# Order of the gate's low-part products and a narrower form of the step-size products in a two-layer decoder kernel

## Chip, cores, metric

The kernel runs on one core of one Trainium2 chip. The metric is the device time of one execution in microseconds; a kernel's time is the median of several runs.

## What is computed

Two layers over 256 tokens of width 1024, in float32, weights used once:

```python
x = x + 0.5 * swiglu(rmsnorm(x, norm_w[l, 0]), gate, up, down)    # hidden 2816
h = rmsnorm(x, norm_w[l, 1])
x = x + mamba2_mixer(h, ...)          # layer 0;  zxbcdt = h @ w_in, the last 32 columns are dt
x = x + swa_sink_attention(h, ...)    # layer 1
x = x + 0.5 * swiglu(rmsnorm(x, norm_w[l, 2]), gate, up, down)
...
dt = softplus(dt_raw + dt_bias)       # step sizes of the 32 heads
```

## The kernel before

Activations stand transposed: eight tiles of 128 features by 256 tokens. Each float32 operand is split into a high part (rounded to float32r) and a low part (the rest, also float32r), and a product is made of three: high by high, high weight by low activation, low weight by high activation. `xs[k]` holds both activation parts side by side, 512 columns: `xh` is the first 256, `xl` the rest. Norm weights are folded into `xs`; the norm's own factor `rs` per token is applied after the products.

Weights come in units of 128 x 1024 (`ORDER` lists all 341 in their order of use). For each, ScalarE writes the high part `hi` (`Weights.high`, L144) and the vector engine the low part `lo` (`Weights.low`, L155). `tick()`, at the end of each unit, first runs what is due in this slot (`Slots`), and then has the parts made up to four units ahead.

A feed-forward stage (f0 to f3, 22 loop steps of 128 hidden columns each, called f) takes per f a gate unit `g`, an up unit `u` and, from f = 4, the down unit `d` of f - 4; the last two down units go together in `tail`. A gate or up unit is `wide`: eight products of 512 columns, high weight by `xs[k]`, and eight of 256 columns, low weight by `xh[k]`, all summed in one PSUM bank; the high weight's product with `xl` is in the bank's second half, and `add` (L514, L515) folds it: ScalarE copies the second half, the vector engine adds the first. In f = 0 the products alternate, in all other f (`by_part`) eight of the one kind follow eight of the other. A down unit (`rows`, L384) is 24 products of 256 columns into the four banks `da`. In f2 two units of the shared K (tile `kab`, 48 products of 256 columns) stand between u and d of f = 5.

At a stage's end `next_stage` updates the residual `X` part by part, ScalarE makes `xh`, the vector engine `xl` (L396), and `rs_stats`, `rs_diag`, `rs_spread` make the norm's factor with small products (tile `st`) between the first units.

The mixer (`ssm`) begins with the unit `dt`: 32 weight columns in a unit of 128, as 24 products of 256 columns in `unit`, in the half of a bank that it shares with the unit B0. `dt_chain` follows in slots: d0 scales it (`dt_raw`), d1 turns it to tokens by rows (`dtt`), d2 and d3 make softplus on four engines, d4 the running sums (`cst`).

Of the kernel before, what the change touches and what calls it, by code (L numbers as in the profile page):

```python
# [9 lines left out]
F32 = mybir.dt.float32  # L10
F32R = mybir.dt.float32r
I32 = mybir.dt.int32
AF = mybir.ActivationFunctionType
ALU = mybir.AluOpType
PSUM = bass.MemoryType.PSUM

P = 128
T = 256
D = 1024
KT = D // P  # L20
# [10 lines left out]
HEADS = 32  # L31
# [44 lines left out]
ORDER = order()  # L76
# [33 lines left out]
class Weights:  # L110
# [38 lines left out]
    def low(self, half=None):  # L149
        u = self.cut  # L150
        c, i = divmod(u, CH)
        if not half:
            self.lo = self.parts.tile([P, D], F32R, tag="lo", name=f"lo{u}")
        hi, lo, s = self.ready.get(u, self.hi), self.lo, self.piece(half)
        self.nc.vector.tensor_tensor(lo[:, s], self.chunks[c][:, i, s], hi[:, s].bitcast(F32), ALU.subtract)  # L155
        if half == 0:
            return
        self.ready[u] = (hi, lo)
        self.cut += 1
        if i == CH - 1 or u == NU - 1:  # L160
            del self.chunks[c]
            self.load()
# [53 lines left out]
class Trunk:  # L216
# [136 lines left out]
            before()  # L353
        self.tick()

    def wide(self, what, out, by_part=False):


        hi, lo = self.W.next(what)
        passes = [(k, w, x, n) for k in range(KT) for w, x, n in ((hi, self.xs, 2 * T), (lo, self.xh, T))]  # L360
        if by_part:
            passes = passes[0::2] + passes[1::2]
        for n, (k, w, x, c) in enumerate(passes):
            self.nc.tensor.matmul(  # L364
                out[:, 0:c], w[:, k * P : (k + 1) * P], x[k],
                start=n == 0, stop=n == len(passes) - 1, skip_group_check=True,
            )
        self.tick()
# [110 lines left out]
    def ffn(self, l, i, key, nxt):  # L479
        nc, wk = self.nc, self.fw  # L480
        self.stage_norm(key)
        accs = self.accs(f"da_{key}")
        hs = {}

        def evac(f, g, u):
            hh = self.op.tile([P, T], F32R, tag="high", name=f"hh_{key}_{f}")
            hl = self.op.tile([P, T], F32R, tag="low", name=f"hl_{key}_{f}")
            hs[f] = (hh, hl)

            def e0():  # L490
                nc.vector.tensor_tensor(g, g, self.rs, ALU.mult)
                nc.scalar.activation(g, g, AF.Silu)
                nc.vector.tensor_tensor(u, u, self.rs, ALU.mult)

            def e1():
                nc.vector.tensor_tensor(u, u, g, ALU.mult)
                nc.scalar.activation(hh, u, AF.Copy)

            def e2():
                nc.vector.tensor_tensor(hl, u, hh.bitcast(F32), ALU.subtract)  # L500

            wait = max(0, 4 - f) if key == "f0" else 2 if f == 0 else 0
            self.slots.chain(wait, [e0, e1, e2])

        def product(name, f, t):

            b = self.bank(f"{name}_{key}_{f}")
            if self.W.pos == 0:
                self.slots.at(0, lambda: nc.scalar.copy(t, b[:, 0:T]))
                self.unit((name, l, i, f), b[:, 0:T])  # L510
                return

            def add():
                nc.scalar.copy(t, b[:, T:])  # L514
                nc.vector.tensor_tensor(t, b[:, 0:T], t, ALU.add)  # L515

            self.slots.at(0, add)
            self.wide((name, l, i, f), b, by_part=f > 0)

        for f in range(NF):  # L520
            g, u = (wk.tile([P, T], F32, tag=n, bufs=4, name=f"{n}s_{key}_{f}") for n in "gu")
            product("g", f, g)
            evac_now = lambda: evac(f, g, u)
            self.slots.late(0, evac_now)
            product("u", f, u)
            if l == 1 and i == 0 and f == 0:
                self.split_k()
            if l == 1 and i == 0 and f == 5:
                self.shared_k()
            if f >= LAG:  # L530
                self.down(l, i, f - LAG, hs, accs)
        for f in range(NF - LAG, NF - 2):
            self.down(l, i, f, hs, accs)
        self.tail([(("d", l, i, f), *hs.pop(f)) for f in (NF - 2, NF - 1)], accs, nxt)
# [15 lines left out]
    def ssm(self, nxt):  # L550
        nc, tc, wk, sl = self.nc, self.tc, self.sw, self.slots
        V, A, G = nc.vector, nc.scalar, nc.gpsimd
        self.stage_norm("ssm")
        causal, ident = self.cc("causal"), self.ident
        H = HEADS
# [6 lines left out]
        def side(name):  # L562

            if sl.now < base + at["so", 0] - 2:
                return self.ps.tile([P, 512], F32, tag="acc", name=name)
            return self.bank(name)
# [3 lines left out]
        yh, yl, sq, R = {}, {}, {}, {}  # L570

        def half():
            if st["n"] % 2 == 0:
                st["bank"] = self.bank(f"sb{st['n']}")
            o = st["bank"][:, (st["n"] % 2) * T : (st["n"] % 2) * T + T]
            st["n"] += 1
            return o
# [28 lines left out]
        def dt_chain(o, d):  # L606

            f = lambda n: wk.tile([P, 2, H], F32, bufs=1, name=n)
            u, t, e, q, p = f("dt"), f("dt_t"), f("dt_e"), f("dt_q"), f("dt_p")
            raw = wk.tile([H, T], F32, bufs=1, name="dt_raw")  # L610
            an = wk.tile([P, H], F32, bufs=1, name="an")
            cs = wk.tile([H, 3 * P], F32, bufs=1, name="cs")
            tok = wk.tile([P, 2, H], F32, bufs=1, name="tok")
            st["dt"], st["tok"] = u, tok

            def d0():
                V.tensor_tensor(raw, o[:H], self.rs[:H], ALU.mult)

            def d1():
                b = st["b"] = side("dtt")  # L620
                for n in range(2):
                    nc.tensor.transpose(b[:, n * H : n * H + H], raw[:, n * P : n * P + P], ident[:H, :H])

            def d2():
                V.tensor_tensor(
                    u, st["b"][:, 0 : 2 * H].rearrange("p (b h) -> p b h", b=2),
                    self.s("dtb", 0, H).unsqueeze(1).broadcast_to([P, 2, H]), ALU.add,
                )
                A.activation(t, u, AF.Abs)
                A.activation(e, t, AF.Exp, scale=-1.0)  # L630
                A.activation(an, self.s("alog", 0, H), AF.Exp)

            def d3():
                G.tensor_scalar(t, e, 2.0, None, ALU.add)
                V.reciprocal(t, t)
                G.tensor_tensor(t, t, e, ALU.mult)
                G.tensor_tensor(q, t, t, ALU.mult)
                V.tensor_scalar(p, q, 2.0 / 15.0, None, ALU.mult)
                for c in (13, 11, 9, 7, 5, 3):
                    V.scalar_tensor_tensor(p, p, 2.0 / c, q, ALU.add, ALU.mult)  # L640
                V.tensor_scalar(p, p, 2.0, None, ALU.add)
                G.tensor_tensor(p, p, t, ALU.mult)
                G.tensor_scalar(u, u, 0.0, None, ALU.max)
                G.tensor_tensor(u, u, p, ALU.add)
                G.tensor_tensor(e, u, an.unsqueeze(1).broadcast_to([P, 2, H]), ALU.mult)
                G.tensor_scalar(e, e, -1.0, None, ALU.mult)

            def d4():
                b = st["b2"] = side("cst")
                for n in range(2):  # L650
                    nc.tensor.matmul(b[:H, n * P : n * P + P], e[:, n], causal, start=True, stop=True)
                for n in range(2):
                    nc.tensor.matmul(b[:, T + n * H : T + n * H + H], causal, e[:, n], start=True, stop=True)
                A.activation(cs[:, 0:P], b[:H, 0:P], AF.Copy, scale=-1.0)
                A.activation(cs[:, T:], b[:H, P:T], AF.Copy, scale=-1.0)
                A.activation(cs[:, P:T], b[:H, P:T], AF.Identity, bias=cs[:, P - 1 : P], scale=-1.0)
                nc.sync.dma_start(scratch, cs)
                A.copy(tok, b[:, T : T + 2 * H].rearrange("p (b h) -> p b h", b=2))

            sl.chain(d, [d0, d1, d2, d3])  # L660
            sl.at(d + 6, d4)

# [162 lines left out]
        for what in seq[:-2]:  # L825
            if what[0] == "so":
                tt = what[1]
                if not accs:
                    accs = self.accs("sa")
                self.rows([(self.W.next(what), yh[tt], yl[tt])], accs, tt == 0, False)  # L830
                self.tick()
            else:
                o = half()
                self.unit(what, o, before=lambda: evac(what, o, E[what] - at[what]), fresh=what == ("dt",))
# [402 lines left out]
```

## Time and profile before

| | |
|---|---|
| three runs, median (lowest to highest) | 1038.58 us (1037.32 to 1039.66) |
| the profiled execution, its own time | 1038.29 us |
| its span, first to last instruction | 1036.5 us, so 1.79 us lie around it |
| busy: PE, vector engine (DVE), ScalarE (ACT), GpSimd (POOL) | 1013.4, 774.7, 627.4, 79.5 us |
| chain that ended last, by line | up 23%, gate 22%, down 22% of the span |
| stages f0, mixer, f1, f2, attention, f3 begin at about | 8, 196, 393, 577, 766, 842 us |

A row of the timeline is a start in us, a length in us, the engine, the line and the operation with output and inputs, and how many were merged into it. A product's record reaches beyond the start of the next one, since products are pipelined: the distance of two starts is what a product costs in a row of products, and the record's length is more.

### The profile page before, as it was taken

How to read it: one execution, taken by the hardware profiler on the slowest of the kernel's cores; microseconds unless marked ns; L12 is line 12 of the kernel's file. 1: busy time of each engine (PE TensorE's matmuls, PEld its weight loads, DVE VectorE, ACT ScalarE, POOL GpSimd, SP SyncE). 2: the span in 40 equal slices, each digit the busy share in tenths (PEclk: the TensorE clock that was granted, in tenths of full speed). 3: DMA queues.
4: the chain of work that ended last, by engine and by line, in shares of the span. 5: the costliest groups of instructions: out<-in, count | busy, mean ns of one | idle time of the engine just before them, and what ended most of it. 6: DMA issues, size and time to landing. Idle time of an engine off the chain costs nothing.

```text
span 1036.5 us, 18344 instructions
## 1 busy us (share of the span) xinstructions
PE 1013.4 (98%) x7290; PEld 939.2 (91%) x7290; DVE 774.7 (75%) x1420; ACT 627.4 (61%) x1106; POOL 79.5 (8%) x122
## 2 busy tenths in 40 slices
PE   8999999999999999999999999999999999999996
PEld 7899999999989898999999899999998888999996
DVE  4866666888999968766667796666679877666665
ACT  6655555678886856555555664555565776555554
POOL 3000000210111112000000200000022020000000
PEclk9999999999999999999999999999999999999998
DMA  8555555547546354555455455555544335545531
GB/s 306 198 203 198 172 203 192 179 177 267 192 153 224 130 199 160 196 198 202 169 203 201 160 203 202 179 200 194 199 181 152 113 141 201 185 181 204 189 117 41
DMA packets 30132, 190.84 MB, mean 184 GB/s; under 512 B 3904, under 2 KB 5728, under 8 KB 8544
## 3 DMA queue, kind: packets, MB, share of 16 engines
q1 hardware_dynamic: 30048, 189.69, 51.5%
q8 instruction: 57, 0.93, 0.3%
q14 instruction: 27, 0.22, 0.1%
HBM read 187.27 MB, written 1.10 MB: 182 GB/s over the span
## 4 chain that ended last, share of the span: by engine, by line
PE 80%; DVE 12%; ACT 3%; DMA 2%; POOL 1%; issue 1%; SPq 0%; DVEq 0%; POOLq 0%
PE u_f L364 23%; PE g_f L364 22%; PE da_f L384 22%; PE sa L384 3%; PE sb L351 3%; DVE lo L155 2%; DVE xs L396 2%; PE aa L384 1%; DMA csb<-cs_scratch 1%; PE q L351 1%; DVE xs L603 1%; DVE X L404 1%; ACT hi L144 1%; DVE E L725 1%; ACT E L720 1%
## 5 line engine op out<-in xcount | busy, mean ns | idle before, releaser
L155 DVE TENSOR_TENSOR lo<-raw,hi 128x1024 fp32r<-128x1024 f32 (+1 forms) x343 | 414.9, 1213 | 15.2 <-ACT hi L144 15.2
L144 ACT ACTIVATE hi<-raw 128x1024 fp32r<-128x1024 f32 (+1 forms) x343 | 357.0, 1046 | 18.6 <-PE da_f L384 5.0
L384 PE MATMUL da_f<-hh_f,hi 128*128 128x256 f32 x704 | 194.3, 276 | 0.0
L384 PE MATMUL da_f<-hh_f,lo 128*128 128x256 f32 x704 | 194.3, 276 | 0.0
L384 PE MATMUL da_f<-hl_f,hi 128*128 128x256 f32 x704 | 194.3, 276 | 0.0
L364 PE MATMUL u_f<-xs,hi 128*128 128x512 f32 x704 | 181.2, 395 | 0.0
L364 PE MATMUL g_f<-xs,hi 128*128 128x512 f32 x696 | 176.6, 392 | 0.8 <-DVE xs L396 0.8
L364 PEld LDWEIGHTS u_f<-xs,hi 128*128 128x128 f32 x704 | 127.1, 188 | 22.4
L364 PEld LDWEIGHTS g_f<-xs,hi 128*128 128x128 f32 x696 | 124.5, 188 | 23.9 <-DVE xs L396 2.2
L384 PEld LDWEIGHTS da_f<-hl_f,hi 128*128 128x128 f32 x704 | 132.1, 188 | 0.0
L384 PEld LDWEIGHTS da_f<-hh_f,hi 128*128 128x128 f32 x704 | 132.1, 188 | 0.0
L384 PEld LDWEIGHTS da_f<-hh_f,lo 128*128 128x128 f32 x704 | 132.1, 188 | 0.0
L515 DVE TENSOR_TENSOR gs_f<-g_f,gs_f 128x256 f32<-128x256 f32 x87 | 37.0, 425 | 108.2 <-ACT gs_f L514 108.2
L364 PEld LDWEIGHTS u_f<-xs,lo 128*128 128x128 f32 x704 | 95.6, 189 | 7.3
L364 PEld LDWEIGHTS g_f<-xs,lo 128*128 128x128 f32 x696 | 95.4, 188 | 6.7
L515 DVE TENSOR_TENSOR us_f<-u_f,us_f 128x256 f32<-128x256 f32 x88 | 37.3, 424 | 85.0 <-ACT us_f L514 85.0
L364 PE MATMUL g_f<-xs,lo 128*128 128x256 f32 x696 | 99.6, 280 | 0.0
L364 PE MATMUL u_f<-xs,lo 128*128 128x256 f32 x704 | 99.6, 278 | 0.0
L514 ACT COPY us_f<-u_f 128x256 f32<-128x256 f32 x88 | 32.7, 372 | 107.5 <-PE u_f L364 107.5
L351 PE MATMUL sb<-xs,hi 128*128 128x256 f32 x656 | 87.0, 283 | 0.3 <-DVE xs L396 0.3
L514 ACT COPY gs_f<-g_f 128x256 f32<-128x256 f32 x87 | 32.2, 370 | 84.1 <-PE g_f L364 84.1
L351 PEld LDWEIGHTS sb<-xs,hi 128*128 128x128 f32 x656 | 80.9, 188 | 1.4 <-issue 0.5
(252 smaller groups left out, 1297.3 us busy)
## 6 DMA issues: line engine op xcount, KB each, us to landing
raw<-w SPq DMA_DIRECT2D x168, 1024.0 KB, 4.9
csb<-cs_scratch SPq DMA_DIRECT2D x8, 768.0 KB, 7.0
raw<-w SPq DMA_DIRECT2D x4, 512.0 KB, 7.7
X<-x SPq DMA_DIRECT2D x4, 256.0 KB, 5.8
Q<-r_q SPq DMA_DIRECT2D x32, 32.0 KB, 1.9
out<-o SPq DMA_DIRECT2D x3, 256.0 KB, 2.2
ca<-const_att SPq DMA_DIRECT2D x1, 704.0 KB, 6.2
raw<-w SPq DMA_DIRECT2D x2, 256.0 KB, 5.8
```

The lines of the kernel that those rows point to most:

```text
L144: self.nc.scalar.activation(hi[:, s], self.chunks[c][:, i, s], AF.Copy)
L155: self.nc.vector.tensor_tensor(lo[:, s], self.chunks[c][:, i, s], hi[:, s].bitcast(F32), ALU.subtract)
L351: nc.tensor.matmul(out, w[:, k * P : (k + 1) * P], x[k], start=n == 0, stop=n == len(passes) - 1)
L364: self.nc.tensor.matmul(out[:, 0:c], w[:, k * P : (k + 1) * P], x[k], start=n == 0, stop=n == len(passes) - 1, skip_group_check=True,)
L384: nc.tensor.matmul(out, w[:, s], x, start=f and j < 4 and m == 0, stop=e and m == 2, skip_group_check=True)
L396: nc.vector.scalar_tensor_tensor(self.xl[j], self.X[j], wcol(j), self.xh[j].bitcast(F32), ALU.mult, ALU.subtract)
L404: nc.vector.scalar_tensor_tensor(self.X[j], out, scale, self.X[j], ALU.mult, ALU.add)
L514: nc.scalar.copy(t, b[:, T:])
L515: nc.vector.tensor_tensor(t, b[:, 0:T], t, ALU.add)
L603: V.scalar_tensor_tensor(out, u[:, tap : tap + T], self.s("convw", tap * 24 + c), out, ALU.mult, ALU.add)
L720: A.activation(e, e, AF.Exp, scale=-1.0)
L725: V.tensor_tensor(f, f, c, ALU.mult)
```

## The change

It has two parts. In gate units the eight low-part products come ahead of the eight 512-column ones (not for the very first unit, nor in f = 0, where they alternate). And the step sizes are made in another form: the 32 low weight columns are written beside the 32 high ones, so that one product has 64 weight columns and all 512 columns of `xs[k]`; eight of them give four quarter results in an own bank from the other group of banks, ScalarE and the vector engine fold the column halves, and a product with two stacked identities (`fold`) folds the row halves while it turns them to tokens.

```diff
     def low(self, half=None):
...
+        if ORDER[u] == ("dt",):
+
+            hi = lo = self.ready[u]
+            cut = lambda x, n: x.rearrange("p (k c) -> p k c", k=KT)[:, :, n * HEADS : (n + 1) * HEADS]
+            self.nc.vector.tensor_tensor(
+                cut(lo, 1), cut(self.chunks[c][:, i], 0), cut(hi, 0).bitcast(F32), ALU.subtract
+            )
...
-    def wide(self, what, out, by_part=False):
+    def wide(self, what, out, by_part=False, low_first=False):
...
         if by_part:
-            passes = passes[0::2] + passes[1::2]
+            passes = passes[low_first::2] + passes[not low_first :: 2]
...
-            self.wide((name, l, i, f), b, by_part=f > 0)
+            self.wide((name, l, i, f), b, by_part=f > 0, low_first=name == "g")
...
-            if st["n"] % 2 == 0:
+            if st["n"] % 2 == 0 or st["n"] == 1:
...
-            raw = wk.tile([H, T], F32, bufs=1, name="dt_raw")
+            raw = wk.tile([2 * H, T], F32, bufs=1, name="dt_raw")
+            fold = wk.tile([2 * H, H], F32, bufs=1, name="dt_fold")
...
             def d0():
-                V.tensor_tensor(raw, o[:H], self.rs[:H], ALU.mult)
+                A.copy(raw, o[: 2 * H, T:])
+                V.tensor_tensor(raw, o[: 2 * H, 0:T], raw, ALU.add)
+                V.tensor_tensor(raw, raw, self.rs[: 2 * H], ALU.mult)
+                V.tensor_tensor(fold, ident[: 2 * H, 0:H], ident[: 2 * H, H : 2 * H], ALU.add)
...
-                    nc.tensor.transpose(b[:, n * H : n * H + H], raw[:, n * P : n * P + P], ident[:H, :H])
+                    nc.tensor.matmul(b[:, n * H : n * H + H], raw[:, n * P : n * P + P], fold, start=True, stop=True)
...
+            elif what == ("dt",):
+                o = side("sbdt")
+                st["n"] += 1
+                hi, _ = self.W.next(what)
+                for k in range(KT):
+                    s = slice(k * P, k * P + 2 * H)
+                    nc.tensor.matmul(o[: 2 * H], hi[:, s], self.xs[k], start=k == 0, stop=k == KT - 1)
+                evac(what, o, E[what] - at[what])
+                self.tick()
```

On PE, stage f0, from the end of a down unit into the gate unit of f = 5, before (out <- moving tile, weight part; then partitions x columns):

```order
L384 MATMUL da_f_208<-hl_f_0_261,hi_393 128x256
L384 MATMUL da_f_208<-hh_f_0_260,lo_421 128x256
L364 MATMUL g_f_5_555<-xs_84,hi_423 128x512
L364 MATMUL g_f_5_555<-xs_85,hi_423 128x512
L364 MATMUL g_f_5_555<-xs_86,hi_423 128x512
```

The same place in the changed kernel:

```order
L392 MATMUL da_f_208<-hl_f_0_261,hi_393 128x256
L392 MATMUL da_f_208<-hh_f_0_260,lo_421 128x256
L372 MATMUL g_f_5_555<-xs_84,lo_452 128x256
L372 MATMUL g_f_5_555<-xs_85,lo_452 128x256
L372 MATMUL g_f_5_555<-xs_86,lo_452 128x256
```

The gate's eight 256-column products now follow the down unit's 24. On PE again, the seam between the same gate unit and its up unit, before:

```order
L364 MATMUL g_f_5_555<-xs_89,lo_452 128x256
L364 MATMUL g_f_5_555<-xs_90,lo_452 128x256
L364 MATMUL g_f_5_555<-xs_91,lo_452 128x256
L364 MATMUL u_f_5_581<-xs_84,hi_456 128x512
L364 MATMUL u_f_5_581<-xs_85,hi_456 128x512
```

And in the changed kernel:

```order
L372 MATMUL g_f_5_555<-xs_89,hi_423 128x512
L372 MATMUL g_f_5_555<-xs_90,hi_423 128x512
L372 MATMUL g_f_5_555<-xs_91,hi_423 128x512
L372 MATMUL u_f_5_581<-xs_84,hi_456 128x512
L372 MATMUL u_f_5_581<-xs_85,hi_456 128x512
```

So sixteen products of 512 columns follow each other, eight of the gate and eight of the up unit, and the up's eight low products come behind them. On PE at the start of the mixer, the end of the unit dt and the norm's first products, before:

```order
L351 MATMUL sb_2211<-xs_90,lo_2058 128x256
L351 MATMUL sb_2211<-xs_91,hi_2031 128x256 x2
L351 MATMUL sb_2211<-xs_91,lo_2058 128x256
L309 MATMUL st_ssm<-ones,ss_n_2104 128x1
L309 MATMUL st_ssm<-ones,sq_n_2186 128x1
```

And in the changed kernel:

```order
L850 MATMUL sbdt<-xs_89,hi_2031 64x512
L850 MATMUL sbdt<-xs_90,hi_2031 64x512
L850 MATMUL sbdt<-xs_91,hi_2031 64x512
L317 MATMUL st_ssm<-ones,ss_n_2103 128x1
L317 MATMUL st_ssm<-ones,sq_n_2185 128x1
```

One product per input tile takes the place of three, and one instead of three needs the last tile, `xs_91`.

## Rows read from the trace of the kernel before

**Rows 1.** The page: busy time by engine, and the chain by engine.

```profile
PE 1013.4 (98%) x7290; PEld 939.2 (91%) x7290; DVE 774.7 (75%) x1420; ACT 627.4 (61%) x1106; POOL 79.5 (8%) x122
...
PE 80%; DVE 12%; ACT 3%; DMA 2%; POOL 1%; issue 1%; SPq 0%; DVEq 0%; POOLq 0%
```

**Rows 2.** The page: granted clock of PE in 40 slices, tenths of full speed.

```profile
PEclk9999999999999999999999999999999999999998
```

**Rows 3.** Timeline of PE, one f of stage f0.

```profile
127.86 1.99 PE L364 MATMUL g_f<-xs,hi 128*128 128x512 f32 x8
129.69 1.11 PE L364 MATMUL g_f<-xs,lo 128*128 128x256 f32 x8
130.63 2.00 PE L364 MATMUL u_f<-xs,hi 128*128 128x512 f32 x8
132.47 1.07 PE L364 MATMUL u_f<-xs,lo 128*128 128x256 f32 x8
133.37 0.28 PE L384 MATMUL da_f<-hh_f,hi 128*128 128x256 f32 x1
...
136.09 1.07 PE L364 MATMUL g_f<-xs,hi 128*128 128x512 f32 x4
```

**Rows 4.** Groups, one product each: gate run's first, second, third; up run's eighth.

```profile
L364 PE MATMUL g_f<-xs,hi 128*128 128x512 f32 x1 | 0.4, 388 | 0.0
...
L364 PE MATMUL g_f<-xs,hi 128*128 128x512 f32 x1 | 0.4, 392 | 0.0
...
L364 PE MATMUL g_f<-xs,hi 128*128 128x512 f32 x1 | 0.4, 394 | 0.0
...
L364 PE MATMUL u_f<-xs,hi 128*128 128x512 f32 x1 | 0.4, 394 | 0.0
```

**Rows 5.** The page's groups: count, busy us, mean ns of one, idle before.

```profile
L384 PE MATMUL da_f<-hh_f,lo 128*128 128x256 f32 x704 | 194.3, 276 | 0.0
```

**Rows 6.** Timeline of PE, stage f3, low parts of u and the next gate.

```profile
854.09 1.10 PE L364 MATMUL u_f<-xs,lo 128*128 128x256 f32 x8
855.03 2.00 PE L364 MATMUL g_f<-xs,hi 128*128 128x512 f32 x8
856.87 1.11 PE L364 MATMUL g_f<-xs,lo 128*128 128x256 f32 x8
```

**Rows 7.** Groups, one product each: last high one before 854.09; first from 855.03.

```profile
L364 PE MATMUL u_f<-xs,hi 128*128 128x512 f32 x1 | 0.4, 388 | 0.0
...
L364 PE MATMUL g_f<-xs,hi 128*128 128x512 f32 x1 | 0.4, 397 | 0.0
```

**Rows 8.** Timeline of PE, stage f2, second down product after K to the gate.

```profile
620.33 0.28 PE L384 MATMUL da_f<-hl_f,hi 128*128 128x256 f32 x1
...
623.03 2.00 PE L364 MATMUL g_f<-xs,hi 128*128 128x512 f32 x8
624.88 0.40 PE L364 MATMUL g_f<-xs,lo 128*128 128x256 f32 x2
```

**Rows 9.** Timeline of PE, stage f0, gate of f = 1; groups, its first two products.

```profile
16.48 2.00 PE L364 MATMUL g_f<-xs,hi 128*128 128x512 f32 x8
18.33 0.28 PE L364 MATMUL g_f<-xs,lo 128*128 128x256 f32 x1
...
L364 PE MATMUL g_f<-xs,hi 128*128 128x512 f32 x2 | 0.6, 397 | 0.0
```

**Rows 10.** Timeline at the mixer's start: vector engine, PE, GpSimd, PE.

```profile
197.83 1.51 DVE L396 SCALAR_TENSOR_TENSOR xs<-X,norms,xs 128x256 fp32r<-128x256 f32 x2
...
199.39 0.38 PE L351 MATMUL sb<-xs,hi 128*128 128x256 f32 x1 [0.25 <-DVE xs L396]
...
221.03 0.43 POOL L646 TENSOR_SCALAR dt_e<-dt_e 128x64 f32<-128x64 f32 x1
...
227.03 0.62 PE L651 MATMUL cst<-co,dt_e 128*32 128x128 f32 x4
```

**Rows 11.** Timeline of ScalarE, the copy in the f of rows 3.

```profile
130.83 0.37 ACT L514 COPY gs_f<-g_f 128x256 f32<-128x256 f32 x1 [1.12 <-PE g_f L364]
```

More of the change, by code (lines that the diff above doesn't have):

```diff
@@ L151, in low @@
         c, i = divmod(u, CH)
[L152 to L155, printed above, removed]
+        if ORDER[u] == ("dt",):
[4 more added lines that the diff above has]
+            )
+        else:
+            if not half:
+                self.lo = self.parts.tile([P, D], F32R, tag="lo", name=f"lo{u}")
+            hi, lo, s = self.ready.get(u, self.hi), self.lo, self.piece(half)
+            self.nc.vector.tensor_tensor(lo[:, s], self.chunks[c][:, i, s], hi[:, s].bitcast(F32), ALU.subtract)
         if half == 0:
```

## Prediction

> **What bounds the kernel now.** I read the page's shares first: PE is busy for 98% of the span, and the chain that ended last lies on PE for 80% of it [rows 1]. The granted clock is full but for the last slice [rows 2]. So a feed-forward stage lasts as long as its products follow each other, and what counts is the spacing from one product's start to the next.
>
> The timeline of one loop step (one f, stage f0) gives it [rows 3]: gate high parts (8 products of 512 columns) 1.83 us, gate low parts (8 of 256) 0.94, up high 1.84, up low 0.90, down (24 of 256) 2.72; with the exact starts behind these rounded ones, 8.233 us. Two products of one size are not spaced alike: the gate's low parts follow at 0.94/8 = 117.7 ns, the up's low parts and the down products at 113.3. A record's busy time runs some 162.5 ns past the next start (276 for the down products [rows 5] against 113.3), so busy time less 162.5 is the spacing of a single product, finer than the timeline's 10 ns.
>
> Read so, a run of 512-column products goes in steps of three. Entered from the 113 pace it shows busy 388, 392, 394, then 388 again [rows 4]: spacing 226, 229, 232, together 687, over and over. The gate's run of eight ends on its second step (392, as the second row), and 256-column products after that go at 117.7. The up's run goes on from there (229, 232, 226, ...) and ends on its third step, 394 [rows 4]; after that they go at 113.3. One stretch of f3 shows the remaining case: up's run ends on the first step, 388 [rows 7], and its low parts go at 0.94/8, 117.5 [rows 6]. A pace, once taken, stays as long as 256-column products follow: after the shared K products the 23 down products from 620.33 to 623.03 go at 117.4 [rows 8], though nothing but their entry differs from other f. So **the step on which a run of 512-column products ends sets the pace of all that follows until the next run.**
>
> **The change, part by part.**
>
> *Gate order.* No product is added. The eight low gate products now follow the down products, and the gate's and up's 512-column runs join to one of sixteen. Entered from the 113 pace: 5 x 687 + 226 = 3.66 us, and sixteen is five rounds and one, so it ends on the first step, and behind that stands the 117.7 pace of [rows 6]. The step's parts: gate low at 113.3, 0.907; run 3.66; up low at 117.7, 0.942; 24 down at 117.7, 2.826. Sum 8.335, 102 ns more than 8.233: the 37 ns that gate's low parts save are spent on up's low parts (35), and 24 x 4.44 = 107 ns are lost on down.
>
> The next step starts at 117.7. Between the two runs lie 8 + 24 + 8 = 40 products in that pace. How does the next run open? Two openings are in the trace. After 8 such products it is one long product of 397 [rows 7]; after 23, again a run of 623.03 to 624.88 as long as that one (1.84; the timeline of rows 6 has 1.84 too) [rows 6, 8]. After a single one (the up unit of f = 0 alternates 512 and 256 columns and ends on one of 256) the first two are long, busy 397 each, then 392, and this run's eighth was 388, the first step [rows 9]. 8 and 23 leave 2 when divided by three, 1 and 40 leave 1. So I take the second opening: eight products 1.842 (16.48 to 18.33 [rows 9], exact starts), ending on the first step, and eight more, 229 + 232 + 2 x 687 = 1.835. That run of sixteen ends on the third step: up low 0.907 and down 2.720 at 113.3 again. With gate low at 0.942 the sum is 8.246, 12 ns more than now. The two kinds of step then alternate: +114 ns for two, +57 for one.
>
> Over a stage: the steps before f = 4 have no down products (-5 and +12 ns by turns); 18 have them; four down units stand behind the last f, at the pace that it left: nothing, or 4 x 107 = 0.43 us. By turns from f = 2 or 3 to 21 that makes +1.02 us where the stage ends at 113 and +1.44 where it ends at 117.7. Which of them cannot be read: the entry follows a wait for the norm's products, and where it restarts is open. At three of the four ends the vector engine, not PE, closes the stage: its normalised inputs come one after another, the last two in 1.51 us from 197.83, and PE waits for them [rows 10]. So of the last 48 products' extra some 0.16 us is hidden there. In f2 the K products set the pace once anew, which leaves 1.2 to 1.3. Sum: f0 1.02 to 1.28, f1 1.03 to 1.29, f2 1.2 to 1.3, f3 1.02 to 1.44, so 4.3 to 5.3; I take **+4.8 us**.
>
> Two covers of this edit. The low part is needed 1.83 us earlier: it comes from the same plan, four units ahead, as the down units' low parts, which are used at their unit's third product and wait for nothing (704 products, idle 0.0) [rows 5]. And ScalarE's copy of the bank's second half starts only at 130.83, after the whole gate unit although that half was done at 129.69 [rows 3, 11]; so finishing both halves together delays nothing.
>
> *Step sizes.* 24 products become 8 of 512 columns. If PE set the time here, 24 x 113.3 - 8 x 229 = 0.89 us would be won. It does not: the last input part is ready at 197.83 + 1.51 = 199.34, and the product that needs it starts at 199.39 [rows 10]. Behind it stood two products (0.35 us to the norm's first product at 199.74, by the timeline), now one (0.23). Gain 0.1, bounds 0 and 0.89; I take 0.1, by the row. The vector engine spares some 0.8 us of low part before the stage's end, where it waits for PE anyway. Later ScalarE gets one copy (0.37, as the copy of [rows 11]), and the vector engine two adds instead of one plus a small one, at most 0.41 more each; ScalarE's copy stands behind a 1.05 us rounding, so the chain starts up to 1.5 us later. Its end on GpSimd is at 221.03 + 0.43, and PE uses it at 227.03 [rows 10]: 5.6 us to spare. Cost 0; without that cover up to 1.9.
>
> Sum: +4.8 - 0.1 = +4.7 on the profiled run's own 1038.29 us, which lies 0.3 under the median of the runs shown: **1043.0 us**.
>
> **A rule against the trace.** The up's and gate's low products have the same 256 columns at 113.3 and 117.7 [rows 3]. The Trainium skill, "TensorE: Matmul & The Clock Gate", section "Back-to-back issue gap", gives a gap by the number of columns alone (N/2.4 + 2.5 ns, an estimate of 109 for 256), and its section "Part 2: What happens when you issue a matmul" says that loading the next weights takes no bandwidth from the running product. By that, order would be free and the gate edit worth 0. This case's trace does not agree: the spacing depends on what ran before.
>
> **Rivals.**
> 1. *Always clean.* The joined run ends so that 113.3 follows; for it: no run of sixteen is in the trace, and a seam between two units could shift the steps. Then gate's low parts win 37 ns in some 80 steps: -3.0 - 0.1, **1035.2**. It decides if a sixteen ends on 394.
> 2. *Always slow.* After 40 products the run opens with one long product as in [rows 7]; then sixteen ends on the first step every time (three, then thirteen). 22 x 107 ns of down in four stages, 9.4, less 0.5 hidden at ends and one unit already slow, up's low parts 2.8, openings 0.9: about 12, **1050.3**.
> 3. *Order is free*, or the paces cancel: only the 0.1, **1038.2**. Against it: 70-odd steps with the same two paces.
> 4. *The step sizes come late*: the 1.9 us above falls on PE in the mixer's full stretch, on top of the forecast: **1045**. Against it the 5.6 us.
>
> **How the numbers follow.** Alternating 0.70; always clean 0.12; always slow 0.10; order free 0.05; late step sizes 0.03. The likeliest gives 1043.0, by itself 1042 to 1044.5. Ends of both signs hold little, so the range takes in the clean case and the late one, leaving out the always slow one: 1035.0 to 1047.0, about 0.9 of the chance; stopping above the clean case would leave less than 0.8. A measurement tells about 0.2% (2.1 us) from no change: slower 0.80 (with some spread at the border), same 0.07, faster 0.13.
>
> **What would show it.** In the profile after: gate low parts of a steady f by turns at busy 276 and 279.5; down products 276 in one f, 279.5 in the next, so a mean of about 278 over their 704 instead of 276; up's low parts with them. The chain still on PE, no wait for low parts in the loop, the norm's first product of the mixer at about 0.1 us less after the last input. Down products all at 276 would prove the first rival, all at 279.5 the second. A PE wait in the mixer for the decay's sums would prove the fourth. Wrong in another way: if the run's steps restart at the seam between gate and up, both units end alike, on the second step, and everything goes at 117.7.

## The result and the profile after

The changed kernel takes 1043.96 us (median of four runs, 1043.67 to 1045.68), against 1039.12 for the kernel before, run beside it on the same chip: a ratio of 1.0052, with a 95% interval of 1.0034 to 1.0070. So it is slower by 4.8 us; 1043.0 had been forecast.

The page after first: busy time by engine, the granted clock in 40 slices, and the chain by engine.

```profile
PE 1019.0 (98%) x7276; PEld 943.7 (91%) x7276; DVE 774.2 (74%) x1422; ACT 627.7 (60%) x1107; POOL 79.9 (8%) x122
...
PEclk9999999999999999999999999999999999999999
...
PE 80%; DVE 12%; ACT 3%; DMA 2%; POOL 1%; issue 1%; SPq 0%; DVEq 0%; POOLq 0%
```

Against [rows 1] the records hold 14 products fewer on PE, and it is busy 5.6 us longer and its weight loads (PEld) 4.5; no other engine moves by more than 0.5. The chain's shares are the same, so no new wait shows in it: the same products are spaced further apart.

Two steps of the loop (two f's) in stage f0, by the timeline of PE after:

```profile
127.28 1.07 PE L372 MATMUL g_f<-xs,lo 128*128 128x256 f32 x8
128.19 1.99 PE L372 MATMUL g_f<-xs,hi 128*128 128x512 f32 x8
130.02 1.99 PE L372 MATMUL u_f<-xs,hi 128*128 128x512 f32 x8
131.85 1.10 PE L372 MATMUL u_f<-xs,lo 128*128 128x256 f32 x8
132.79 0.28 PE L392 MATMUL da_f<-hh_f,hi 128*128 128x256 f32 x1
...
135.62 1.10 PE L372 MATMUL g_f<-xs,lo 128*128 128x256 f32 x8
136.56 2.00 PE L372 MATMUL g_f<-xs,hi 128*128 128x512 f32 x8
138.40 2.00 PE L372 MATMUL u_f<-xs,hi 128*128 128x512 f32 x8
140.24 1.07 PE L372 MATMUL u_f<-xs,lo 128*128 128x256 f32 x8
141.14 0.28 PE L392 MATMUL da_f<-hh_f,hi 128*128 128x256 f32 x1
...
143.86 1.07 PE L372 MATMUL g_f<-xs,lo 128*128 128x256 f32 x8
```

Take the differences of the starts. The first step is gate low 0.91, the joined run 3.66, up low 0.94, down 2.83: 8.34 us, where the prediction had 0.907, 3.66, 0.942, 2.826. The second is 0.94, 3.68, 0.90, 2.72: 8.24, where it had 0.942, 1.842 + 1.835, 0.907, 2.720. Before, a step of the loop took 8.23 [rows 3].

The single products at the turning points, after: the last of the first joined run (at 131.8 us), the first two of the second (from 136.56), and its last (at 140.2):

```profile
L372 PE MATMUL u_f<-xs,hi 128*128 128x512 f32 x1 | 0.4, 388 | 0.0
...
L372 PE MATMUL g_f<-xs,hi 128*128 128x512 f32 x2 | 0.6, 397 | 0.0
...
L372 PE MATMUL u_f<-xs,hi 128*128 128x512 f32 x1 | 0.4, 394 | 0.0
```

So the first run ends on the first step of three, the second opens with two long products and ends on the third step.

The down products of these two steps, one input pair each (lengths are minimum, median, maximum in ns; the first row is from the step at 132.79, the second from the one at 141.14):

```profile
L392 PE MATMUL da_f<-hh_f,hi x8: 280/280/280, 132.8 to 135.3; 128*128 128x256 f32 x8
...
L392 PE MATMUL da_f<-hh_f,hi x8: 276/276/276, 141.1 to 143.5; 128*128 128x256 f32 x8
```

In one step all 24 are at 279 to 280, in the next all at 276, and so by turns through all four stages (in f2 the K products make it two slow units running at the start, and the four units behind the last f keep the pace that it left). The page's group shows the mean of both:

```profile
L392 PE MATMUL da_f<-hh_f,lo 128*128 128x256 f32 x704 | 195.5, 278 | 0.0
```

Down was 276 before [rows 5], and its idle time is still 0.0. The low products of gate and up are at a mean of 278 too, with no idle time: the low parts that the gate now wants earlier were in time.

Where the time lies is read by windows from the first down product of a stage to the last (the window, its length, PE's busy time in down products with their count, the granted clock, the DMA share, GB/s). Before, for f0, f1, f2, f3:

```profile
42.81:196.37 153.56, 62.60 (x528) 1.00 0.56 196
422.99:576.56 153.57, 62.61 (x528) 1.00 0.57 199
606.21:765.66 159.45, 62.71 (x528) 1.00 0.56 200
871.58:1025.16 153.58, 62.61 (x528) 1.00 0.46 161
```

and after:

```profile
41.66:196.66 155.00, 63.98 (x528) 1.00 0.55 195
424.63:579.63 155.00, 63.98 (x528) 1.00 0.55 197
609.24:770.12 160.88, 64.09 (x528) 1.00 0.56 198
875.94:1030.54 154.60, 63.56 (x528) 1.00 0.45 160
```

The four stretches grow by 1.44, 1.43, 1.43 and 1.02 us, 5.3 together, at full clock in both kernels. The spans differ by 5.4 (1041.9 against 1036.5). What lies between the stretches differs too, but cancels. The largest differences lie in the loop's entry in f0 and at the mixer's start; windows around them show what clock was granted there. Before:

```profile
20.00:27.00 7.00, 6.57 (x30) 0.76 0.78 294
196.00:205.00 9.00, 8.75 (x75) 1.00 0.33 117
```

and after:

```profile
20.00:27.00 7.00, 6.68 (x40) 1.00 0.83 320
196.00:205.00 9.00, 8.15 (x48) 0.81 0.33 117
```

Apart from the kernel's end, where PE has no products left, each of these two executions has one stretch in which the lower of the two clock levels was granted, 1.2 GHz, behind waits of PE: before at f0's entry (the 40 slices of [rows 2] are too coarse to show it), after at the mixer's start (0.50 from 201.60 to 204.80). Up to f0's first down product the kernel after is 1.15 us ahead (41.66 against 42.81); from f0's last down product to f1's first gate product it takes 198.49 us, 1.25 more than before. The slow stretch in the mixer does not always come with the new step sizes: the run of the step sizes alone, below, was granted 1.00 from 196 to 205.

The mixer's start after, in the timelines of three engines (vector engine, PE, GpSimd, PE):

```profile
197.96 1.50 DVE L404 SCALAR_TENSOR_TENSOR xs<-X,norms,xs 128x256 fp32r<-128x256 f32 x2
...
199.79 0.28 PE L317 MATMUL st_ssm<-ones,ss_n 128*128 128x1 f32 x2
...
222.93 0.43 POOL L658 TENSOR_SCALAR dt_e<-dt_e 128x64 f32<-128x64 f32 x1
...
228.94 0.30 PE L663 MATMUL cst<-co,dt_e 128*32 128x128 f32 x1
```

From the end of the last input part, 197.96 + 1.50 = 199.46, to the norm's first product it is 0.33 us; it was 199.34 to 199.74, 0.40 [rows 10]. The decay's chain ends on GpSimd at 223.36 and PE uses it at 228.94, 5.6 us later, the same to spare as before.

### The profile page after: what moved, and what is told of

Read it like the earlier page. It is cut to its first block, busy times and chain, and to the rows that moved or that the text cites. A ratio compares the mean times of both kernels' runs of the same rounds, so it can differ in the third digit from the quotient of the medians.

```text
span 1041.9 us, 18326 instructions
## 1 busy us (share of the span) xinstructions
PE 1019.0 (98%) x7276; PEld 943.7 (91%) x7276; DVE 774.2 (74%) x1422; ACT 627.7 (60%) x1107; POOL 79.9 (8%) x122
## 4 chain that ended last, share of the span: by engine, by line
PE 80%; DVE 12%; ACT 3%; DMA 2%; POOL 1%; issue 1%; SPq 0%; DVEq 0%; POOLq 0%
PE u_f L372 23%; PE da_f L392 22%; PE g_f L372 22%; PE sa L392 3%; PE sb L359 3%; DVE lo L163 2%; DVE xs L404 2%; PE aa L392 1%; DVE xs L611 1%; PE q L359 1%; DVE X L412 1%; DMA csb<-cs_scratch 1%; ACT hi L144 1%; DVE E L737 1%; ACT E L732 1%
## 5 line engine op out<-in xcount | busy, mean ns | idle before, releaser
L372 PEld LDWEIGHTS u_f<-xs,hi 128*128 128x128 f32 x704 | 132.2, 188 | 28.6
L372 PEld LDWEIGHTS g_f<-xs,lo 128*128 128x128 f32 x696 | 88.3, 188 | 0.2
L359 PE MATMUL sb<-xs,hi 128*128 128x256 f32 x640 | 84.8, 285 | 0.0
L500 ACT ACTIVATE gs_f<-gs_f 128x256 f32<-128x256 f32 x88 | 36.8, 419 | 71.9 <-DVE gs_f L499 71.9
```

The source lines that it names most:

```text
L359: nc.tensor.matmul(out, w[:, k * P : (k + 1) * P], x[k], start=n == 0, stop=n == len(passes) - 1)
L372: self.nc.tensor.matmul(out[:, 0:c], w[:, k * P : (k + 1) * P], x[k], start=n == 0, stop=n == len(passes) - 1, skip_group_check=True,)
```

## The experiments

One theory was tested: the spacing of 256-column products is set by what PE ran before them, by the step on which the last 512-column run ended and, as the fourth experiment and those behind it showed, by how a stage is entered. The rivals were that the low part ahead costs something in itself, that two joined runs do, and that spacing goes by columns alone. "Loop stretch" in the table is the time from the first down product's start to the last one's in each stage, by the exact starts of the profiled execution; that of the kernel before is 153.45, 153.45, 159.33 and 153.45 us. The difference of medians is against the runs of before made beside each kernel.

| kernel | loop stretch f0, f1, f2, f3, us | sum less before | median less before | ratio (95%) |
|---|---|---|---|---|
| the change | 154.88, 154.88, 160.77, 154.48 | +5.3 | +4.8 | 1.0052 (1.0034 to 1.0070) |
| gate order alone | 154.48, 154.48, 160.77, 154.88 | +4.9 | +4.5 | 1.0043 (1.0030 to 1.0056) |
| step sizes alone | 153.45, 153.45, 159.33, 153.45 | 0.0 | +0.2 | 0.9999 (0.9991 to 1.0008) |
| up low first instead | 155.92, 155.92, 161.67, 156.01 | +9.8 | +8.7 | 1.0082 (1.0067 to 1.0096) |
| six low, eight high, two low | 153.00, 156.25, 159.05, 156.25 | +4.9 | +5.7 | 1.0053 (1.0038 to 1.0068) |
| both low first | 155.80, 155.80, 161.50, 153.45 | +6.9 | +7.3 | 1.0076 (1.0062 to 1.0091) |
| six, eight, two after settling | 153.00, 153.00, 158.93, 153.00 | -1.8 | -1.4 | 0.9986 (0.9978 to 0.9995) |
| no wide products after settling | 152.21, 152.21, 158.23, 152.21 | -4.8 | -5.8 | 0.9945 (0.9933 to 0.9956) |
| settled by two f's, then narrow | 152.28, 152.28, 158.38, 152.28 | -4.5 | -5.1 | 0.9950 (0.9938 to 0.9962) |
| run of fifteen | 152.77, 152.77, 158.73, 152.77 | -2.6 | -3.1 | 0.9967 (0.9954 to 0.9980) |
| narrow without settling | 158.17, 158.17, 163.94, 158.18 | +18.8 | +20.0 | 1.0189 (1.0175 to 1.0204) |

The sums of one profiled execution and the medians of several runs agree to 1.2 us; the rest lies outside the loops. One thing that differs there from execution to execution is the stretch at the lower clock.

DMA traffic can be left out as the cause. In the fourth experiment f0 is fast at a DMA share of 0.56 and f3 slow at 0.45; in the fifth f0 is slow at 0.55 and f3 fast at 0.46.

A count by the exact starts in all twelve profiled executions bears out the first half of the theory. It takes, at full clock, each run of at least two 512-column products with four or more of 256 columns behind it and no wait near its end. Of 605 runs that end on the third step, 603 go on at 113 ns (one of the other two stands ahead of 48 products of another kind, the K products in f2). Of 578 that end on the first or the second step, none does; 575 go on at 117 to 118.

**Gate order alone.** The diff of the change without `dt`:

```diff
-            passes = passes[0::2] + passes[1::2]
+            passes = passes[low_first::2] + passes[not low_first :: 2]
...
-            self.wide((name, l, i, f), b, by_part=f > 0)
+            self.wide((name, l, i, f), b, by_part=f > 0, low_first=name == "g")
```

> The gate order alone, the step sizes as before. Pace theory (the step of three on which a run of 512-column products ends sets the spacing of the 256-column products behind it): the loss is all here, +4.8 us to before (+4.3 to +5.3), down products by turns at busy 276 and 279 from one f to the next. Rival (part of the loss comes from the step sizes' longer chain in the mixer): clearly under +4.8, say +3.

1043.06 us, +4.5: the loss is in this edit (+4.8 with both, the intervals overlap). The down units go by turns, as in the change. Here f0 and f1 end at 276, f2 and f3 at 279; in the change it was f3 alone that ended at 276. So the end a stage falls on is not fixed by the order.

**Step sizes alone.** The change with `low_first=False` in both units.

> The step sizes alone, the gate as before. Pace theory: -0.1 us, that is within 0.03% of before, all down products at busy 276 as before, the last input of the mixer to the norm's first product about 0.1 us shorter. Rival (the chain starts later and PE waits in the mixer): +1 to +2 us, with a PE wait at cst or y that before does not have.

1038.7 us, +0.2, inside the interval of no change; every loop stretch is that of before. The edit does nothing that can be measured.

**Up low first instead of the gate's.**

```diff
+            self.wide((name, l, i, f), b, by_part=f > 0, low_first=name == "u")
```

> Low products first in the up units instead of the gate units, so that the runs stay eight long with sixteen 256-column products between the gate's and the up's, and the down products follow a run of 512. Pace theory, worked out step by step from the spacings of the trace of before: both runs then end on a step that leaves the down products at busy 279 in every f, none by turns; +150 to +163 and +71 ns by turns, about +117 per f, +9.9 us in all. Rival (low parts first cost what they cost in the gate): about +4.8 us, down products by turns. Rival (order is free): 0.

1047.18 us, +8.7; the loop stretches, +9.8, are the forecast almost to the tenth. One step in its timeline:

```profile
120.44 2.00 PE L364 MATMUL g_f<-xs,hi 128*128 128x512 f32 x8
...
122.29 1.10 PE L364 MATMUL g_f<-xs,lo 128*128 128x256 f32 x8
123.23 1.10 PE L364 MATMUL u_f<-xs,lo 128*128 128x256 f32 x8
...
128.84 0.39 PE L364 MATMUL g_f<-xs,hi 128*128 128x512 f32 x1
```

The step takes 8.40 us, and both low parts go at the slow pace (0.94 us for eight, records of 1.10). Up's run is now followed at once by down, and down stays slow in every f of every stage. The same products in another order cost nearly twice what the change costs.

**Six low products, eight high, two low.** The gate's run gets two 256-column products behind it, so that up's run is entered apart.

```diff
-            passes = passes[0::2] + passes[1::2]
+            high, low = passes[0::2], passes[1::2]
+            passes = low[:n_low] + high + low[n_low:]
...
+            self.wide((name, l, i, f), b, by_part=f > 0, n_low=6 if name == "g" else 0)
```

> Gate: six low products, eight of 512 columns, then two low products; up and down as before, so the two runs of eight stay apart, by two products in place of eight. Pace theory: the two between them go at 120 and 117.5, the next run then opens on the same step as in before, so the six in front, the up's low parts and the down products all go at 113.3: -27 ns in each of some 80 steps, -2.2 us. Rival (low parts ahead of the run are what costs): +2 to +5 us. Rival (order is free): 0.

1044.22 us, +5.7: the forecast missed. The trace shows how. The down products of f0 and of f1 (lengths as minimum, median, maximum):

```profile
L385 PE MATMUL da_f<-hh_f,hi x175: 276/276/276, 43.3 to 195.7; 128*128 128x256 f32 x175
...
L385 PE MATMUL da_f<-hh_f,hi x176: 279/279/279, 422.6 to 578.7; 128*128 128x256 f32 x176
```

In f0 it is as worked out, 0.45 us below before; in f1 and f3 not one down product of a whole stage is at 276; in f2 the first two units are at 279 and all behind the K products at 276. What had been left out is the entry: this order can repeat in two ways, and by itself does not leave the one in which it starts. The order of before brought its own slow entry back: in its f0 up's low parts take 0.94 us in f = 2 (30.83 to 31.77), behind the norm's products, and 0.90 from f = 3 on (36.39 to 37.29). The single runs spread from 1040.8 to 1046.7 us, which fits entries that fall differently each time; only the profiled execution shows its stages, so that is argued. The next runs tested the entry.

**Both low first, every f from 1 on.** `low_first=True` in both units.

> Gate and up products both low part first from f = 1 on, step sizes as before. So each 512-column run again has 256-column products on both sides, as before. Theory (each product's spacing depends on what ran before it): a stage that enters the settled stretch in the 113.3 ns pace stays there, 8233 ns per f, no change; a stage that enters it in a slow pace either comes back within one f or stays slow for its whole length, 8340 ns per f, which is 107 ns x about 18 = 1.9 us for such a stage. So 1038.5 with no slow stage, up to 1046 with four, and within a stage all down units are alike (276, or 279 to 280), never by turns. Rival (low part first costs something in itself, 4.5 us for the gate): 1043 + the same again for up, 1047, with the down units by turns or mixed in all four stages. Rival (order is free, 1038.5 and all at 276).

1045.2 us, +7.3, with runs from 1043.1 to 1047.9. The down products of f1 and of f3:

```profile
L384 PE MATMUL da_f<-hh_f,lo x176: 279/279/279, 423.2 to 578.7; 128*128 128x256 f32 x176
...
L384 PE MATMUL da_f<-hl_f,hi x176: 276/276/276, 876.4 to 1029.6; 128*128 128x256 f32 x176
```

f0 and f1 are slow from end to end, f2 is slow behind its first down unit and the K products, and f3 is 153.45 us, that of before to the last digit, with low parts first in every unit. So the low part ahead costs nothing in itself: one code, two patterns, by the entry. The median alone could have passed for the rival's. (A slow stage costs 2.35 us, not the 1.9 expected: all 22 down units are slow, not 18.)

A slow stage is not slow in all its products. One step of f0, its gate's and its up's low parts:

```profile
127.52 1.10 PE L364 MATMUL g_f<-xs,lo 128*128 128x256 f32 x8
...
130.29 1.07 PE L364 MATMUL u_f<-xs,lo 128*128 128x256 f32 x8
```

Up's eight go at 113 here and the gate's at 118; in f3 it is the other way round (0.91 us for the gate's, 0.94 for up's). In either stage one of the two runs of eight ends on the third step. Where it is the gate's, the eight low products of up gain by it; where it is up's, the 24 down products and the gate's low ones do.

**Six, eight, two after settling.** As the fourth run, with `n_low=6` only from f = 4 on (f = 7 in f2).

> The gate order of six low products, eight high ones, two low ones again, but only from f = 4 on (f = 7 in f2); the f's ahead of it in the order of before. It asks why the first form of this order was slower. Theory: its gain of 26 ns per f is real, and in two of the four stages it was lost since they entered in a slow pace, which this order keeps and the order of before mends within one f. With the first f's in the order of before every stage should be at 276 in its down units and each later f 8207 instead of 8233 ns: 26 x 69 = 1.8 us less, 1036.7. If before's order does not mend the entry in a stage, that stage is at 8367, 134 x 18 = 2.4 us more. Rival (the two low products between the runs cost something of themselves): 1044 again, with f's longer than 8233 ns everywhere.

1036.56 us, -1.4 (loop stretches -1.8, as worked out). All stages are at 276 but for one unit in f2, the one behind the K products, which is at 279 before too. The same order that had cost 5.7 us wins once it is entered right.

**No wide products.** Each 512-column product as two of 256 columns from f = 4 on (f = 7 in f2).

```diff
+            halves = lambda k: [(k, hi, self.xh, 0, T), (k, hi, self.xl, T, 2 * T)]
+            passes = (sum([halves(k) for k in range(KT)], []) if narrow else high) + low
```

> From f = 4 on (f = 7 in f2) each 512-column product of gate and up is issued as two 256-column ones, same weights twice, same sums; the f's ahead as before. There is then no 512-column run in these f's that could change the pace, and no step of 226, 229, 232 ns. Theory: a stage that comes in at 113.3 ns keeps it to its end: 72 products x 113.3 = 8160 ns per f, 73 less than before, x 69 = 5.0 us less, 1033.5 in all; a stage that comes in slow would keep 117.7 for all, 8480 per f, +247 x 18 = 4.4 us for that stage (each down unit at 279 to 280). Rival (spacing depends on columns alone, or a second weight load per product costs time): 32 more issues per f at not less than before's mean, 1038.5 or slower.

1032.15 us, -5.8, for -5.0 forecast, runs from 1032.05 to 1032.58; the loop stretches give -4.8 of it. One step:

```profile
126.27 1.98 PE L366 MATMUL g_f<-xs,hi 128*128 128x256 f32 x16
128.09 1.07 PE L366 MATMUL g_f<-xs,lo 128*128 128x256 f32 x8
128.99 1.98 PE L366 MATMUL u_f<-xs,hi 128*128 128x256 f32 x16
130.81 1.07 PE L366 MATMUL u_f<-xs,lo 128*128 128x256 f32 x8
...
134.43 0.39 PE L366 MATMUL g_f<-xs,hi 128*128 128x256 f32 x2
```

8.16 us. Sixteen narrow products take 1.82 us where eight wide ones took 1.83 or 1.84, and all low parts are at 0.90 to 0.91. The win of 73 ns a step is gate's low parts and the steps of the wide run; the second weight load for each narrow pair costs nothing that can be seen.

**Settled by two f's, then narrow.** One f in the order of before, one with both low first, narrow from there.

```diff
+            passes = low + high if mode == 1 else (narrow if mode > 1 else high) + low
...
+            self.wide((name, l, i, f), b, by_part=f > 0, mode=f - (7 if (l, i) == (1, 0) else 4))
```

> As the run without wide products, but the second f after the settling ones (f = 5, in f2 f = 8) has both gate and up low part first, and the narrow products begin with f = 6 (f = 9 in f2). By the theory worked on all four paces in which a stage can enter, one f in before's order and then one with the low part first in both bring every one of them to 113.3 ns; so the narrow part is never entered slow: 61 f's x 73 = 4.5 us less, 1034.1, with the same result in every run and all down units at 276 from f = 6 on. Rival (low part first is itself what costs): the one f in each stage sets the pace to 117.7 for the whole rest, +247 x 61 = 15 us, 1053.

1032.82 us, -5.1. That f with both low first does no harm, and the result is as good as the last within the intervals. That it is also the safer one was not shown: in no profiled stage, of this run or the last, did the narrow products begin at the slow pace.

**Run of fifteen.** The change's gate order, but up's last wide product in halves, from f = 4 on (f = 7 in f2).

```diff
+            if mode == "g":
+                passes = low + high
+            elif mode == "u":
+                passes = high[:-1] + halves(KT - 1) + low
```

> Gate low part first as in the change, but the last of up's eight 512-column products is issued as two of 256 columns, so that the joined run has fifteen, five full rounds of three, and ends on the third step. From f = 4 on (f = 7 in f2), the f's ahead in the order of before, so that a stage comes in at 113.3 ns. Step sizes as before. Theory: every down unit at 276, 8193 instead of 8233 ns per f, 40 x 69 = 2.8 us less than before, 1035.2; a stage that comes in on one of the slow paces would be at 8193 as well or, at worst, at 8393 (+2.9 us for that stage, all its down units at 279 to 280). Rival (the gate's low part first, or two runs joined, costs time in itself): 1043 as in the change, with units by turns at 276 and 279 or all at 279. Rival (spacing goes by columns alone): 1038.

1035.28 us, -3.1, for 1035.2 forecast. One step (the row of nine in up holds seven wide ones and, merged with them, the two of 256 columns):

```profile
126.55 1.07 PE L371 MATMUL g_f<-xs,lo 128*128 128x256 f32 x8
127.46 1.99 PE L371 MATMUL g_f<-xs,hi 128*128 128x512 f32 x8
129.29 1.99 PE L371 MATMUL u_f<-xs,hi 128*128 128x512 f32 x9
131.12 1.07 PE L371 MATMUL u_f<-xs,lo 128*128 128x256 f32 x8
...
134.75 0.50 PE L371 MATMUL g_f<-xs,lo 128*128 128x256 f32 x3
```

8.20 us. This is the sharpest of the tests: one product fewer in the joined run, five full rounds of three instead of five and one, and the change's loss becomes a gain. Low part first and two joined runs are both still there. The run differs from the change in its first f's too, but these do not explain it: in the change as well, f0 and f1 come to their first down unit at 276, and behind the next joined run of sixteen the second unit is at 279, where here it stays at 276.

**Narrow without settling.** The narrow form from f = 1 on.

> No 512-column products from f = 1 on: the narrow form of the run without wide products, without the f's in the order of before ahead of it. Nothing is left in a stage that could bring a slow entry back, since the entry follows waits and behind it stand 256-column products only. Theory: a stage is at one pace from its entry to its end, all its down units alike. After waits the mixer's 256-column products of the earlier runs go on at 117.7, so most or all stages should be slow: 8480 ns per f, +247 x 18 = 4.4 us and more for each slow stage, 1055 with four slow ones; a stage entered at 113.3 gives 8160 and wins 1.3 to 1.6. Rival (the narrow form wins by itself, whatever ran before): 1031 to 1032, as with the settling f's. Rival (the win of the narrow form came from elsewhere, the paces are a by-product): the time does not go with the count of slow stages.

1058.32 us, +20.0, where 1055 had been worked out for four slow stages. All down products of one input pair in the whole kernel (the other two pairs are alike):

```profile
L386 PE MATMUL da_f<-hh_f,hi x704: 279/280/283, 42.1 to 1044.1; 128*128 128x256 f32 x176
```

All four stages are slow: nothing in them brought the pace back. From f = 4 on (f = 7 in f2) the instructions are those of the run at 1032.15; f = 1 to 3 of each stage (1 to 6 in f2) decide over 26 us, 23.6 of them in the loop stretches.

## Why the prediction was right

*Gate order, +4.8 forecast.* The steps of three, the joined run's end on the first step, the opening with two long products after 40 at 117.7, and the alternation all stand in the rows after, part by part to the timeline's 10 ns. Under it lay one guess: that the way in which a run opens goes by the number of products ahead of it, counted by threes, read off three openings alone; the run behind the 40 bore it out. The size depended on one thing left open, the pace on which each stage ends: +1.02 us at 113, +1.44 at 117.7. Three of the four ended slow, and the stretches grew by 1.44, 1.43, 1.43 and 1.02. At f0's end the vector engine hid 0.15 of it, as allowed for (0.16): its last input part stands 155.02 us behind the first down product before (197.83 - 42.81) and 156.30 after (197.96 - 41.66), +1.28, the upper bound given for f0. f2 was given at most 1.3 for its K products and grew by 1.43: that term was too small by 0.1. The edit alone measured +4.5.

The prediction's rule is too wide in one place, the K products of f2, which it priced (one unit at the slow pace) but did not explain. Up's low parts ahead of them go at 113 (613.54 to 614.45, 0.91 us), and the K products, in records of 283 ns against 276, at 120, with no 512-column run between:

```profile
L351 PE MATMUL kab<-xkl,hi x16: 283/283/283, 615.4 to 619.1; 128*128 128x256 f32 x16
```

So the last step of a run does not set the pace of all that follows until the next run: 256-column products of another kind changed it. Why these do is open.

*Step sizes, -0.1 and no late cost.* 0.33 for 0.40 us at the mixer's first norm product, 5.6 us to spare on the decay's chain; alone, a ratio of 0.9999. Not PE but the last input part sets the time there, so 16 products fewer won nothing.

*The rivals.* Always clean is out, but only just: with one product fewer in the run, and first f's in the order of before, all is clean but for the unit behind the K products. Always slow is out for this order, and all down units slow is what up low first gives. Late step sizes are out by the experiment on them alone. Order is free is out most widely: the same products took from 1036.6 to 1047.2 us by order alone. The rule of the Trainium skill that had spoken for it ("TensorE: Matmul & The Clock Gate", section "Back-to-back issue gap") goes by the columns alone and gives, as an estimate, 109 ns for 256 of them; the section calls this the gap of an isolated matmul, and says that in a stream the weight loads bear on the spacing too. The trace does not agree with a gap by columns alone, since the spacing is 113.3 or 117.7 ns by what ran ahead. *Restart at the seam* is out by the alternation: it would have left every down unit slow.

*Where luck had a part.* The prediction took one entry for all stages and needed no more, since under the change's order each pace gives way to the other within one step, whatever the entry. The fourth experiment, worked out from a single entry in the same way, failed on that. That the median meets the forecast to less than 1 us is luck in part as well: three stages ended slow here, two in the gate order alone, and single runs of the kernel before differ by 2.7 us (1037.32 to 1039.97).

What remains open: why the spacing goes in steps of three and keeps a pace, which no row shows; and which entry leads to which pace, since the norm's waits end differently from run to run. The traces give a first hint. In f = 0, where up's products alternate, its low products go in one of two patterns: 118, 119 and 120 ns in turn, or 118, 118 and 123. In both low first, the two stages with the first pattern (f0, f1) came in slow and the two with the second (f2, f3) fast. It is not the whole answer: in six low, eight high, two low all four have the first pattern, and f0 was fast. The settling f's in the order of before brought all 16 stages of the four kernels that have them into the fast pace, from either pattern.

## What to carry to other kernels

Where PE is busy to 98% and waits for nothing, look at the spacing of its products, not at their count: group the rows by shape, and if one shape shows two lengths (276 and 279 here), ask what ran ahead of each. A reordering that frees nothing and moves nothing can still shift the pace of thousands of products behind it, and whether it wins can hang on the count in a run; try neighbours of the count, and look at each stage by itself, since a median mixes paces. In this kernel a few settling steps ahead of a loop that keeps its pace were enough to bring it into the fast one.

## What the runs showed that had not been expected

The pace of the down products lasts: 22 units of 24, with gate and up between them, from end to end at 279 or at 276, in one and the same code (both low first, f1 against f3: 155.80 and 153.45 us). Among 256-column products alone no way back was seen: narrow without settling loses 4.7 us in a stage that, settled, wins 1.2.

A 512-column product was not cheaper than two of 256 columns: 229 ns in the mean against 226.7 (twice 113.3), although the pair loads its weights twice.

The mixer's products of 256 columns go on at some 117.7 (a median record of 279 ns before, from 205 to 342 us); nothing in this study tried to bring those to 113.3.
